# Attention without row maxima: a runtime bound on the scores, a factor table in place of bias matmuls, and a branch to the general program

## The chip, the cores and the metric

The kernel runs on one core of a Trainium2 chip. A core has TensorE (PE, matmuls; PEld is its weight loads), VectorE (DVE), ScalarE (ACT), GpSimd (POOL) and SyncE (SP, which issues most DMAs). Matmuls read SBUF and write PSUM, which has eight banks of 512 float32 columns here. The metric is device microseconds of one launch; lower is better.

## The reference

One encoder layer on x of 1024 tokens by 1024, float32. One projection gives q, k, v of two head groups, which run side by side; then an output projection, and a gated MLP with a depthwise convolution over positions.

```python
def rms_norm(x, g): return x * rsqrt(mean(x * x) + 1e-6) * g

# mixer A: 8 query heads, 2 key heads of 64, all 1024 keys
qa, ka = rope(rms_norm(qa, qa_norm_g)), rope(rms_norm(ka, ka_norm_g))
p = softmax(qa @ ka.T / 8);  out_a = p @ va
# mixer B: 8 heads; patterns (window, dilation) (128,1), (512,4), (2048,16), merged by their denominators
sc = rms_norm(qb, qb_norm_g) @ rms_norm(kb, kb_norm_g).T / 8 - slope[h] * distance      # -1e30 outside
w = softmax(logsumexp of each pattern);  out_b = sum of w * softmax(sc) @ vb
x = x + concat(rms_norm(out_a), rms_norm(out_b)) @ w_out
x = x + conv_ffn(rms_norm(x))
# qa_norm_g, ka_norm_g, qb_norm_g, kb_norm_g: 64 values each, 1 + 0.05 * normal
```

After the norms a q or k vector of 64 is no longer than 8 times its largest gain, so a score is at most 8 times the product of the two largest gains.

## The kernel before

The kernel is written with the Tile framework: Python emits the operations in an order written out by hand, and the framework's planner then sets each engine's queue, and may move an operation ahead of others. SBUF is two arenas, `bigf` (float32) and `bigr` (fp32r, the format of the fast matmuls), addressed by fixed offsets; PSUM is `ps`. For precision an operand is split into a high and a low fp32r part, and a product is the sum of high x high, high x low and low x high.

The stages follow one another in time: the input projection (to about 208 us), mixer A (208 to 426), mixer B (426 to about 578, its end mixed with the output projection), the output projection to about 665, the up-projection with convolution and gate, and the down-projection.

**Mixer A** takes 16 groups `g`, each one block of 128 positions and one key head, whose four query heads make 512 columns. `a_main` walks eight key tiles `kt`: two score matmuls of 512 columns (lines 664 and 665) into bank 2 or 3, an exp on ACT from PSUM to SBUF (667), and two tiles later the product with V (line 659, plain float32, four pieces, each two passes in the trace). Between them it takes the next group's preparation from a list: `nat` (split of q, 616 and 617), `first` (four transposes and a copy), `mx(i)` four times, and `last`, which turns the maxima into columns. The weights of line 664 stack K's high and low part in 128 partitions against q's high part twice; those of line 665 stack K's high part with rows of -1 against q's low part and the row maximum, so the score arrives with its maximum subtracted. Transposes all show at line 177 or 180.

```python
635  for hf in range(2):
637      mm(bank(hf), r(q2 + 128 * i, 128), r(R_K2A + 1024 * kv + 512 * hf, 512), start=True, stop=True)
638      vec.tensor_reduce(f(SM_MC + 8 * hf + i, 1), bank(hf), axis=AX.X, op=OP.max)
```

**Mixer B** takes 8 heads of 8 steps `s` in one loop: `b_s(h, s)` makes scores, `b_pv` two steps later the product with V. Steps 0 to 3 are banded (near keys that are not a multiple of 4 away), steps 4 to 7 strided (keys 4 apart, all three patterns together, each key counted as often as it occurs). A bias matmul with the identity (line 793) first writes the table of distance penalties, `tbc`, into the bank; then two pairs of 256-column score matmuls (805 and 807, or 815 and 816), again with the maximum in the second; an exp in PSUM (819); for banded steps a high part (ACT, 821) and a low part (DVE, 822), for strided steps a product with the count table `cnt` (824). Sums of V products are gathered at 844 and 848 and normalised at 684 and 685. In the same steps run the next head's preparation: `b_split` (split of k and q, 720, 721, 616, 617), `trq` and `trk` (transposes and copies), `mx(tt)` eight times (a 432-column and a 256-column product, lines 753 to 758, each with a masked maximum on DVE against the table `tmx`, line 764), and `trl` (772 to 777). Head 0's preparation runs in A's last two groups.

```python
793  bias = lambda o, rhs, first: mm(o, r(R_IDR, 128), rhs, start=first, stop=False, skip_group_check=True)
819  act(bank(st), bank(st), AF.Exp)
821      act(r(ph, 512), bank(st), AF.Copy)
822      vec.tensor_tensor(r(pl, 512), bank(st), rf(ph, 512), op=OP.subtract)
824      vec.tensor_tensor(heads(f(p, 512), 2), heads(bank(st), 2), fp(F_CNT, [128, 2], [1, 256]), op=OP.mult)
```

`load_tmx` (SP queue, 672 KB) and `load_tabs` (POOL queue, 384 KB) fetch the two tables once a head. POOL also copies K's high part to other partitions by a DMA (740).

Of the kernel before, what the change touches and what calls it, by code (L numbers as in the profile page):

```python
# [20 lines left out]
HD = 64  # L21
# [19 lines left out]
NF = O_F + 9232  # L41
# [49 lines left out]
F_CNT = O_F + 8720  # L91

# [31 lines left out]
def tile_encoder_layer(ctx, tc, x, w_in, gains, outg, norm1_g, norm2_g, w_out, w_up, conv_w, conv_b,  # L124
                       w_down, ident, rope, tmx, tbc, cnt, out):
# [13 lines left out]
    act = nc.scalar.activation  # L139
    vec = nc.vector  # L140
    gp = nc.gpsimd
    mm = nc.tensor.matmul
    dma = nc.sync.dma_start

    def f(off, n):
        return bigf[:, off:off + n]

    def r(off, n):
        return bigr[:, off:off + n]

    def rf(off, n):
        return bigr[:, off:off + n].bitcast(F32)

    def raw_ap(base, dims):
        return bass.AP(tensor=base.tensor, offset=base.offset,
                       ap=[list(base.ap[0])] + [list(d) for d in dims])

    def fp(off, *dims):
        return raw_ap(bigf[:, off:off + 1], dims)

    def rp(off, *dims):
        return raw_ap(bigr[:, off:off + 1], dims)

    def rfp(off, *dims):
        return raw_ap(bigr[:, off:off + 1].bitcast(F32), dims)

    def pp(off, *dims):
        return raw_ap(PS[:, off:off + 1], dims)

    def bank(i, n=512, o=0):  # L170
        return PS[:, 512 * i + o:512 * i + o + n]

    def heads(ap, n):
        return ap.rearrange("p (h d) -> p h d", h=n)

    def tr_r(b, slot, src):
        nc.tensor.transpose(bank(b, 128, 128 * slot).bitcast(F32R), src, r(R_IDR, 128))

    def tr_f(b, slot, src):
        nc.tensor.transpose(bank(b, 128, 128 * slot), src, f(O_IDF, 128))  # L180

    def perm_rows(t, b, width):
        rr, c = divmod(b, 2)
        return bass.AP(tensor=t.tensor, offset=t.offset + (512 * c + rr) * width, ap=[[4 * width, 128], [1, width]])

    def bcast(t, n, off=0):
        return bass.AP(tensor=t.tensor, offset=t.offset + off, ap=[[0, 128], [1, n]])

    def newton(dst, v, root, t):

        vec.reciprocal(root, root)
        vec.tensor_tensor(t, root, root, op=OP.mult)
        vec.scalar_tensor_tensor(t, t, -0.5, v, op0=OP.mult, op1=OP.mult)
        vec.scalar_tensor_tensor(dst, t, 1.5, root, op0=OP.add, op1=OP.mult)

    trb = [0]

    def next_tr():
        trb[0] ^= 1
        return 4 + trb[0]  # L200

    def evac_split(o, b, n=512):
        act(r(o, n), bank(b, n), AF.Copy)
        vec.tensor_tensor(r(o + 1024, n), bank(b, n), rf(o, n), op=OP.subtract)

    def xt(tt):
        return R_XT + 2048 * tt

    def qab(tt):
        return O_QAB + 1024 * tt  # L210

    def fill(dst, n, m, c, src=O_IDF, eng=None):

        src = f(src, m)[:, None, :].to_broadcast([128, n, m])
        if eng is None:
            vec.tensor_scalar(dst, src, 0.0, c, op0=OP.mult, op1=OP.add)
        else:
            act(dst, src, AF.Copy, scale=0.0, bias=c)
# [5 lines left out]
    INW = 2304  # L224
    chunks = [(1280, "kb"), (1792, "vb"), (0, "qa"), (768, "qb")]
    prods = [(c, n) for c in range(4) for n in ((1, 5, 2, 7, 6, 3, 4) if c else (1, 2, 5, 7, 6, 3, 4))]

    def a_op(n, t):
        return R_A[n] + 1024 * t

    def split(o, src):
        act(r(o, 512), src, AF.Copy)
        vec.tensor_tensor(r(o + 512, 512), src, rf(o, 512), op=OP.subtract)

    def x_bank(tt):
        return 4 + 2 * (tt % 2)

    def x_prep(tt):
        for half in range(2):
            b = x_bank(tt) + half  # L240
            for k in range(4):
                tr_f(b, k, f(qab(tt) + 512 * half + 128 * k, 128))
            split(a_op(((1, 2), (3, 4))[tt // 4][half], tt % 4), bank(b))

    def x_rest(tt):
        q0, q1 = qab(tt % 4), qab(tt % 4 + 4)
        b = x_bank(tt), x_bank(tt) + 1
        act(f(F_JNK, 512).bitcast(BF), f(qab(tt), 1024), AF.Square, accum_out=f(SM_SS1 + tt, 1))
        vec.tensor_scalar(f(SM_E1 + tt, 1), f(SM_SS1 + tt, 1), EPS / D, EPS * EPS, op0=OP.mult, op1=OP.add)
        if tt < 4:  # L250
            for half in range(2):
                act(f(q0 + 512 * half, 512), bank(b[half]), AF.Copy)
        else:
            act(f(q1, 512), bank(b[0]), AF.Copy)
            vec.tensor_tensor(f(q1 + 512, 512), f(q0, 512), bank(b[0]), op=OP.subtract)
            vec.tensor_tensor(f(q1, 512), bank(b[1]), f(q1, 512), op=OP.add)
            gp.tensor_tensor(f(q0, 512), f(q1, 512), f(q0, 512), op=OP.subtract)
            gp.tensor_tensor(f(q0 + 512, 512), f(q0 + 512, 512), f(q0, 512), op=OP.subtract)

    def s_split(n, t):  # L260
        raw = {5: qab(t + 4), 7: qab(t + 4) + 512, 6: qab(t), 3: qab(t) + 512}[n]
        split(a_op(n, t), f(raw, 512))


    def kv_load(half):
        src = bass.AP(tensor=w_in.tensor, offset=w_in.offset + 512 + 512 * half * INW,
                      ap=[[INW, 128], [128 * INW, 4], [1, 256]])
        dma(heads(f(F_WC + 1024 * half, 1024), 4), src)

    def kv_split(k):  # L270
        o, raw, g = R_A[7] + 2048 * (k // 4) + 256 * (k % 4), f(F_WC + 256 * k, 256), f(SM_G1 + k, 1)
        act(r(o, 256), raw, AF.Copy, scale=g)
        vec.scalar_tensor_tensor(r(o + 1024, 256), raw, g, rf(o, 256), op0=OP.mult, op1=OP.subtract)

    def kv_bank(tt):
        return tt if tt < 4 else 2 + tt % 2

    def kv_proj(tt):
        for k in range(8):
            a = a_op(((1, 2), (3, 4))[tt // 4][k // 4], tt % 4) + 128 * (k % 4)  # L280
            w = R_A[7] + 2048 * (k // 4) + 256 * (k % 4)
            o = bank(kv_bank(tt), 256)
            mm(o, r(a, 128), r(w, 256), start=(k == 0), stop=False)
            mm(o, r(a, 128), r(w + 1024, 256), start=False, stop=False)
            mm(o, r(a + 512, 128), r(w, 256), start=False, stop=(k == 7))

    def rot(dst, qn, nh, tab):
        for half in range(2):
            gp.tensor_tensor(fp(dst + 16 * half, [64, nh], [32, 2], [1, 16]),
                             fp(qn + 16 * (1 - half), [64, nh], [32, 2], [1, 16]),  # L290
                             fp(tab + 64 + 16 * half, [0, nh], [32, 2], [1, 16]), op=OP.mult)

    def kv_out(i):
        stg = F_KVT + 256 * (i % 3)
        act(f(stg, 256), bank(kv_bank(i), 256), AF.Copy)  # L295
        dma(kvscr[i], f(stg, 256))


    def k_fetch():
        dma(heads(f(F_TMP, 1024), 8), kvscr[:, :, 0:128].rearrange("t p c -> p t c"))  # L300

    def k_norm():
        k3, t = heads(f(F_TMP, 1024), 16), F_KSQ + 1024
        act(f(F_KSQ, 1024), f(F_TMP, 1024), AF.Square)
        vec.tensor_reduce(f(t, 16), heads(f(F_KSQ, 1024), 16), axis=AX.X, op=OP.add)
        vec.scalar_tensor_tensor(fp(t + 16, [2, 8], [1, 2]), fp(t, [2, 8], [1, 2]), 1.0 / HD,
                                 fp(SM_E1, [1, 8], [0, 2]), op0=OP.mult, op1=OP.add)
        act(f(t + 32, 16), f(t + 16, 16), AF.Sqrt)
        newton(f(t, 16), f(t + 16, 16), f(t + 32, 16), f(t, 16))
        vec.tensor_tensor(k3, k3, f(t, 16)[:, :, None].to_broadcast([128, 16, 64]), op=OP.mult)  # L310
        vec.tensor_tensor(k3, k3, fp(O_GA + 128, [0, 16], [1, 64]), op=OP.mult)

    def k_turn():
        for ax in range(2):
            for half in range(2):
                gp.tensor_tensor(fp(F_KSQ + 32 * ax + 16 * half, [128, 8], [64, 2], [1, 16]),
                                 fp(F_TMP + 32 * ax + 16 * (1 - half), [128, 8], [64, 2], [1, 16]),
                                 fp(F_ROPE + 64 + 32 * ax + 16 * half, [128, 8], [0, 2], [1, 16]), op=OP.mult)

    def k_add():  # L320
        k4 = fp(F_TMP, [128, 8], [64, 2], [1, 64])
        vec.tensor_tensor(k4, k4, fp(F_ROPE, [128, 8], [0, 2], [1, 64]), op=OP.mult)
        vec.tensor_tensor(f(F_TMP, 1024), f(F_TMP, 1024), f(F_KSQ, 1024), op=OP.add)
# [815 lines left out]
    for t in tail:  # L1139
        t()  # L1140
# [433 lines left out]
```

## Time and profile before

| | |
|---|---|
| median of 3 runs | 1325.74 us (1324.68 to 1325.79) |
| span of the profiled execution | 1324.9 us (its own time beyond the span is not given) |
| granted TensorE clock, mean | 0.998 |
| PE / DVE / ACT / POOL busy | 1298.4 / 1013.5 / 682.2 / 387.2 us |
| mixer A, window 208 to 426 | PE busy 218.0, DVE 131.0, ACT 112.9 us |
| mixer B, window 426 to 578 | PE busy 145.4, DVE 117.5, ACT 112.5 us |

A row of a group of instructions reads: line, engine, operation, output<-input by the program's names, shape of output<-input, xcount | busy us, mean ns of one | idle time of the engine just before them and what ended it. A matmul's duration overlaps the next one's, so its cost on the queue is the distance to the next start. A row of the timeline starts with the start in us and the length in us. A row of a window lists busy time and count of each engine, then the granted clock, the DMA share and GB/s.

### The profile page before, as it was taken

How to read it: one execution, taken by the hardware profiler on the slowest of the kernel's cores; microseconds unless marked ns; L12 is line 12 of the kernel's file. 1: busy time of each engine (PE TensorE's matmuls, PEld its weight loads, DVE VectorE, ACT ScalarE, POOL GpSimd, SP SyncE). 2: the span in 40 equal slices, each digit the busy share in tenths (PEclk: the TensorE clock that was granted, in tenths of full speed). 3: DMA queues.
4: the chain of work that ended last, by engine and by line, in shares of the span. 5: the costliest groups of instructions: out<-in, count | busy, mean ns of one | idle time of the engine just before them, and what ended most of it. 6: DMA issues, size and time to landing. Idle time of an engine off the chain costs nothing.

```text
span 1324.9 us, 20107 instructions
## 1 busy us (share of the span) xinstructions
PE 1298.4 (98%) x7559; PEld 1127.1 (85%) x7559; DVE 1013.5 (76%) x1599; ACT 682.2 (51%) x1070; POOL 387.2 (29%) x304
## 2 busy tenths in 40 slices
PE   8999999999999999999999999999999999999998
PEld 7999999999999888878877888888888888888887
DVE  4987687556655777866588999999999999586674
ACT  8855564555545777773465444444544445244331
POOL 1611122000111222100115667656766653100000
PEclk9999999999999999999999999999999999999999
DMA  7145211001002455333222222322232225897873
GB/s 259 53 113 127 81 44 48 17 1 35 4 9 66 98 141 143 97 118 111 82 70 88 103 104 103 111 96 97 88 119 104 104 95 191 307 309 232 293 232 104
DMA packets 120500, 152.28 MB, mean 115 GB/s; under 512 B 50962, under 2 KB 77010, under 8 KB 119890
## 3 DMA queue, kind: packets, MB, share of 16 engines
q1 hardware_dynamic: 118609, 143.65, 33.3%
q0 software_dynamic: 1792, 7.34, 2.5%
q8 instruction: 59, 0.97, 0.3%
q14 instruction: 40, 0.32, 0.1%
HBM read 112.95 MB, written 33.82 MB: 111 GB/s over the span
## 4 chain that ended last, share of the span: by engine, by line
PE 77%; DVE 14%; issue 4%; ACT 4%; DMA 1%; SPq 0%; DVEq 0%; ACTq 0%
PE ps L659 8%; DVE bigf L1288 6%; PE ps L1255 6%; PE ps L1257 6%; PE ps L1256 6%; PE ps L1387 5%; PE ps L1386 5%; PE ps L1388 5%; PE ps L411 3%; PE ps L412 3%; PE ps L413 3%; PE ps L664 3%; PE ps L637 2%; PE ps L665 2%; DVE bigf L1259 2%
## 5 line engine op out<-in xcount | busy, mean ns | idle before, releaser
L1255 PE MATMUL ps<-bigr 128*128 128x512 f32 x616 | 241.6, 392 | 6.3 <-DVE bigf L1259 5.7
L1256 PE MATMUL ps<-bigr 128*128 128x512 f32 x616 | 240.4, 390 | 0.0
L1257 PE MATMUL ps<-bigr 128*128 128x512 f32 x616 | 240.3, 390 | 0.0
L1288 DVE SCALAR_TENSOR_TENSOR bigf<-bigf 128x768 f32<-128x768 f32 (+1 forms) x176 | 178.7, 1073 | 26.5 <-ACT bigf L1286 26.3
L1238 ACT ACTIVATE bigr<-bigf 128x512 fp32r<-128x512 f32 x154 | 93.2, 625 | 139.2 <-POOL bigf L1230 70.3
L659 PEld LDWEIGHTS ps<-bigf 128*128 128x128 f32 x1024 | 139.9, 191 | 10.3
L1255 PEld LDWEIGHTS ps<-bigr 128*128 128x128 f32 x616 | 116.0, 188 | 35.0 <-DVE bigf L1259 9.1
L1366 ACT ACTIVATE bigr<-bigf 128x1024 fp32r<-128x1024 f32 x77 | 80.7, 1060 | 119.1 <-PE ps L1388 65.7
L1257 PEld LDWEIGHTS ps<-bigr 128*128 128x128 f32 x616 | 116.0, 188 | 24.4
L1256 PEld LDWEIGHTS ps<-bigr 128*128 128x128 f32 x616 | 116.0, 188 | 23.6
L659 PE MATMUL ps<-bigf 128*128 128x65 f32 x1024 | 135.2, 267 | 0.0
L411 PE MATMUL ps<-bigr 128*128 128x256 f32 x448 | 127.2, 284 | 1.2 <-ACT bigf L295 1.2
L1239 DVE TENSOR_TENSOR bigr<-bigf,bigr 128x512 fp32r<-128x512 f32 x112 | 125.2, 1135 | 3.2 <-ACT bigr L1238 2.7
L412 PE MATMUL ps<-bigr 128*128 128x256 f32 x448 | 126.8, 283 | 0.0
L413 PE MATMUL ps<-bigr 128*128 128x256 f32 x448 | 126.7, 283 | 0.0
L667 ACT ACTIVATE bigf<-ps 128x512 f32<-128x512 f32 x128 | 76.0, 597 | 94.5 <-PE ps L665 93.4
L1387 PE MATMUL ps<-bigr 128*128 128x512 f32 x308 | 119.9, 389 | 0.0
L1388 PE MATMUL ps<-bigr 128*128 128x512 f32 x308 | 119.8, 389 | 0.0
L1386 PE MATMUL ps<-bigr 128*128 128x512 f32 x308 | 119.8, 389 | 0.0
L1367 DVE TENSOR_TENSOR bigr<-bigf,bigr 128x1024 fp32r<-128x1024 f32 x77 | 93.0, 1222 | 27.1 <-ACT bigr L1366 23.2
L638 DVE TENSOR_REDUCE bigf<-ps 128x1 f32<-128x512 f32 x128 | 86.3, 690 | 23.5 <-PE ps L637 21.6
L411 PEld LDWEIGHTS ps<-bigr 128*128 128x128 f32 x448 | 85.8, 192 | 1.9 <-ACT bigf L295 1.6
(233 smaller groups left out, 2860.2 us busy)
## 6 DMA issues: line engine op xcount, KB each, us to landing
bigf<-w_down SPq DMA_DIRECT2D x99, 256.0 KB, 4.5
bigf<-w_up SPq DMA_DIRECT2D x44, 512.0 KB, 3.6
bigf<-gscr SPq DMA_DIRECT2D x77, 256.0 KB, 4.2
gscr<-bigf SPq DMA_DIRECT2D x33, 512.0 KB, 2.6
bigf<-w_in SPq DMA_DIRECT2D x8, 1024.0 KB, 5.2
bigf<-x SPq DMA_DIRECT2D x15, 512.0 KB, 6.5
bigf<-tmx SPq DMA_DIRECT2D x8, 672.0 KB, 5.2
bigf<-w_out SPq DMA_DIRECT2D x8, 512.0 KB, 5.9
```

Of the source, the lines that this page charges most:

```text
L411: mm(o, ah, wh, start=(k == 0 and t % 2 == 0 and n != 2), stop=False, skip_group_check=True)
L412: mm(o, ah, wl, start=False, stop=False, skip_group_check=True)
L413: mm(o, al, wh, start=False, stop=(k == 3), skip_group_check=True)
L659: mm(bank(ob, 65, 66 * i), f(slots[kt] + 128 * i, 128), f(F_VA + 132 * kt + 66 * kv, 65), start=(kt == 0 and i == 0), stop=(kt == 7), skip ...
L1239: (gp if n in (2, 4) and m > 3 else vec).tensor_tensor(rp(o + 512, [128, 4], [1, 128]), src, rfp(o, [128, 4], [1, 128]), op=OP.subtract)
L1255: mm(bank(b), wh, th, start=(k == 0 and n in (1, 5, 6, 7)), stop=False, skip_group_check=True)
L1256: mm(bank(b), wh, tl, start=False, stop=False, skip_group_check=True)
L1257: mm(bank(b), wl, th, start=False, stop=(k == 3), skip_group_check=True)
L1288: vec.scalar_tensor_tensor(f(a + o, n), f(i + d, n), w_, f(a + o, n), op0=OP.mult, op1=OP.add)
L1386: mm(o, ah, r(d, 512), start=(q == 0 and n in (1, 5, 2)), stop=False, skip_group_check=True)
L1387: mm(o, ah, r(d + 1024, 512), start=False, stop=False, skip_group_check=True)
L1388: mm(o, al, r(d, 512), start=False, stop=(q == NQ - 1), skip_group_check=True)
```

## The change

The body of the program becomes a function, emitted twice: `emit(True)`, and, behind a branch at run time, `emit(False)`, which is the program of before. `emit(True)` works out from the gains the square of a bound on any score, 64 times the larger of max(qa gain squared) x max(ka gain squared) and max((qb gain x kb gain) squared), and leaves maxima out: exp of the bare scores. If the bound exceeds 256 (scores over 16), it multiplies the q gains by 0, so that nothing overflows, and the branch at its end runs the general program over it.

- **Scores.** K is stacked as low and high part, q as high and low part, so the first score matmul gives low x high and high x low; the second is high x high, its other 64 weight rows zero. The counts of matmuls stay, `mx`, `last`, `trl`, the bias matmuls and the transposes of the maxima go. `k_ready` moves K's high part down by a POOL DMA instead of an ACT copy.
- **Tables.** `tee` = exp(`tbc`) times the counts, 768 columns a head, loaded in two halves of 192 KB on SP's queue. One DVE product after exp replaces the bias matmul and, in strided steps, the count product. In banded steps it writes float32 to SBUF; high part (`tensor_copy`) and low part both follow on DVE.
- **Banks.** Score banks rotate over 2, 3, 0, 1 instead of 2, 3.
- Three output weights load to another place, since `tee` lies where they lay.

The diff, without its whitespace and cut:

```diff
+    def emit(bounded):
 def k_split():
-    act(rp(R_KNA, [128, 16], [1, 64]), src, AF.Copy)
-    vec.tensor_tensor(rp(R_KNA + 64, ...), src, rfp(R_KNA, ...), op=OP.subtract)
+    h, l = (64, 0) if bounded else (0, 64)
+    act(rp(R_KNA + h, [128, 16], [1, 64]), src, AF.Copy)
+    vec.tensor_tensor(rp(R_KNA + l, ...), src, rfp(R_KNA + h, ...), op=OP.subtract)
 def k_ready(u):
     act(rp(R_K2A + 256 * u, [128, 2], [1024, 2], [1, 128]), pb, AF.Copy)
+    if bounded:
+        gp.dma_start(rp(R_KHA + 256 * u, [1024, 2], [1, 256])[0:64], rp(R_K2A + 256 * u, [1024, 2], [1, 256])[64:128])
+        return
     act(rp(R_KHA + 256 * u, [128, 2], [1024, 2], [1, 128])[0:64], pb[0:64], AF.Copy)
+def bound():
+    t = F_UA
+    vec.tensor_tensor(fp(t, [64, 2], [1, 64]), fp(O_GA, [128, 2], [1, 64]), fp(O_GA, [128, 2], [1, 64]), op=OP.mult)
+    vec.tensor_tensor(f(t + 128, 64), f(O_GB, 64), f(O_GB + 64, 64), op=OP.mult)
+    vec.tensor_tensor(f(t + 128, 64), f(t + 128, 64), f(t + 128, 64), op=OP.mult)
+    vec.tensor_reduce(f(t + 192, 3), heads(f(t, 192), 3), axis=AX.X, op=OP.max)
+    vec.tensor_tensor(f(t + 192, 1), f(t + 192, 1), f(t + 193, 1), op=OP.mult)
+    vec.tensor_tensor(f(t + 192, 1), f(t + 192, 1), f(t + 194, 1), op=OP.max)
+    vec.tensor_scalar(f(O_LIM, 1), f(t + 192, 1), float(HD), None, op0=OP.mult)
+    vec.tensor_scalar(f(O_LIM + 1, 1), f(O_LIM, 1), LIMIT, None, op0=OP.is_le)
 def late_consts():
+    if bounded:
+        bound()
...
+            vec.tensor_scalar(f(g, 64), f(g, 64), HD ** -0.5, f(O_LIM + 1, 1), op0=OP.mult, op1=OP.mult)
+def q_pair(src, stride, eng, n, o):
+    q = fp(src, [stride, n], [1, 64])
+    act(rp(R_QD + o, [128, n], [1, 64]), q, AF.Copy)
+    eng.tensor_tensor(rp(R_QD + 64 + o, [128, n], [1, 64]), q, rfp(R_QD + o, [128, n], [1, 64]), op=OP.subtract)
 def a_prep(g):
+    if bounded:
+        return [nat, first]
     return [nat, first] + [lambda i=i: mx(i) for i in range(4)] + [last]
 def a_main(g, prep, tail, late, plan, late_plan):
-        st = 2 + kt % 2
+        st = (2, 3, 0, 1)[kt % 4] if bounded else 2 + kt % 2
-        mm(bank(st), r(R_KHA + 1024 * kv + 128 * kt, 128), r(ql, 512), start=False, stop=True)
+        mm(bank(st), r(R_KHA + 1024 * kv + 128 * kt, 128), r(q2 if bounded else ql, 512), start=False, stop=True)
+def load_tee(h, part):
+    if bounded and h < 8:
+        dma(f(F_TEE[part], 384), tee[h][:, 384 * part:384 * part + 384])
 def b_prep(h):
+    if bounded:
+        return [[L(trq, 0)], [L(trk, 0), L(trk, 1)]], \
+            [[L(trq, 1)], [], [], [], [L(b_split, h + 1) if h < 7 else None], [], [], []]
+def b_s_bounded(h, s):
+    st = (2, 3, 0, 1)[s % 4]
...
+        for i, k in enumerate(ks):
+            mm(o, r(k, 128), q, start=(u == 0 and i == 0), stop=(i == 1), skip_group_check=True)
+    p, ph, pl = b_slots[h, s] = p_slots()
+    act(bank(st), bank(st), AF.Exp)
+    if s >= 4:
+        vec.tensor_tensor(heads(f(p, 512), 2), heads(bank(st), 2), fp(tb, [128, 2], [1, 256]), op=OP.mult)
+        return
+    at = [ta + win(2 * s + u) - 32 * (2 * s + u) + 32 for u in range(2)]
+    if at[0] == at[1]:                                   # s = 1, 2
+        vec.tensor_tensor(fp(p, [256, 2], [64, 4], [1, 64]), pp(512 * st, [256, 2], [64, 4], [1, 64]),
+                          fp(at[0], [0, 2], [96, 4], [1, 64]), op=OP.mult)
+    else:                                                # s = 0, 3
+        for u in range(2):
+            vec.tensor_tensor(fp(p + 256 * u, [64, 4], [1, 64]), pp(512 * st + 256 * u, [64, 4], [1, 64]),
+                              fp(at[u], [96, 4], [1, 64]), op=OP.mult)
+    vec.tensor_copy(r(ph, 512), f(p, 512))
+    vec.tensor_tensor(r(pl, 512), f(p, 512), rf(ph, 512), op=OP.subtract)
 # the loop of mixer B
         b_s(h, s)
+        if s == 4:
+            load_tee(h + 1, 0)
+        if s == 0 and h:
+            load_tee(h, 1)
...
+emit(True)
+limit = nc.values_load(bigf[0:1, O_LIM:O_LIM + 1].bitcast(mybir.dt.int32), ...)
+with tc.If(limit > int(np.float32(LIMIT).view(np.int32)), preferred_fallthrough_block=False):
+    emit(False)
```

More of the change, by code (lines that the diff above doesn't have):

```diff
@@ L158, in fp @@
[L158 to L177, printed above, removed]
@@ L245, in x_rest @@
[L245 to L258, printed above, removed]
@@ L287, in rot @@
[L287 to L300, printed above, removed]
@@ L313, in k_turn @@
[L313 to L323, printed above, removed]
@@ new lines, in emit @@
+        last = NPAIR - 1
+        for m in range(len(steps)):
+            n, q = steps[m]
+            down(m)
+            d_prep(m + 3)
+            if m < 2:
+                conv(last, m)
+            if m == 2:
+                gate(last, 0)
+                gate(last, 1)
+            if m == 3:
+                take(gate_sums(last), 4)
+            d_load2(m + 6)
+            d_load(m + 7)
+            behind(n, q)
+    emit(True)
+    limit = nc.values_load(bigf[0:1, O_LIM:O_LIM + 1].bitcast(mybir.dt.int32), min_val=0, max_val=2 ** 31 - 1,
+                           skip_runtime_bounds_check_because="any float32 that is not negative is right")
```

2257 lines of the change are left out of this document (1163 added, 1094 removed).

## The prediction

> **What bounds the kernel now.** I read the page first: the busy line and the chain of waits.
>
> ```profile
> PE 1298.4 (98%) x7559; PEld 1127.1 (85%) x7559; DVE 1013.5 (76%) x1599; ACT 682.2 (51%) x1070; POOL 387.2 (29%) x304
> ...
> PE 77%; DVE 14%; issue 4%; ACT 4%; DMA 1%; SPq 0%; DVEq 0%; ACTq 0%
> ```
>
> TensorE holds 98% of the span and 77% of the chain. The change cuts TensorE work out of two stages, so I next asked for busy time by window: mixer A (208 to 426), one head of mixer B (464 to 483), the last head, and everything from the up-projection on, which the change leaves alone.
>
> ```profile
> 208.00:426.00 218.00, 218.00 (x1574) 200.32 (x1573) 130.96 (x268) 112.91 (x192) 23.62 (x27) 1.00 0.08 22
> 464.00:483.00 19.00, 18.33 (x141) 16.13 (x140) 14.86 (x49) 13.67 (x26) 4.96 (x5) 1.00 0.50 128
> 559.00:578.00 19.00, 17.51 (x119) 14.61 (x118) 14.25 (x22) 15.17 (x26) 0.00 (x0) 1.00 0.40 125
> 665.00:1325.00 660.00, 647.70 (x2845) 531.42 (x2842) 549.44 (x617) 282.70 (x368) 275.86 (x194) 1.00 0.44 147
> ```
>
> The columns are PE, PEld, DVE, ACT and POOL busy. In A, TensorE never rests and the others are at 60% or less: a matmul removed is time removed. In a B head TensorE has 18.33 of 19.00 us, but DVE has 14.86 and ACT 13.67, so what is saved there ends where one of these takes over. The granted clock is 1.00 in all four.
>
> The profiled execution spans 1324.9 us; its own time beyond the span is not given, but the runs' median is 1325.74, so some 0.8 us lies around a span. I subtract from the median. About 0.2% (2.6 us) is what a measurement can tell from no change.
>
> **Mixer A.** Removed per group: eight max matmuls (line 637) with their DVE reductions (638), and four of eight transposes (643) with one ACT copy. The scores stay at two matmuls per key tile. The timeline of TensorE shows what a key tile costs:
>
> ```profile
> 303.64 0.48 PE L664 MATMUL ps<-bigr 128*128 128x512 f32 x1
> 303.96 0.40 PE L665 MATMUL ps<-bigr 128*128 128x512 f32 x1
> 304.19 0.63 PE L637 MATMUL ps<-bigr 128*128 128x512 f32 x2
> 304.65 1.00 PE L659 MATMUL ps<-bigf 128*128 128x65 f32 x8
> 305.46 0.47 PE L664 MATMUL ps<-bigr 128*128 128x512 f32 x1
> ```
>
> Durations overlap, so I count from start to start. From 303.64 to 305.46 is 1.82 us; the two max matmuls hold 304.19 to 304.65, 0.46; without them a tile is 1.36 us. Four transposes I read from
>
> ```profile
> 493.55 0.54 PE L177 MATMUL ps<-bigr 128*128 128x128 f32 x4 [0.67 <-DVE bigr L772]
> 493.92 0.35 PE L758 MATMUL ps<-bigr 128*128 128x256 f32 x1
> ```
>
> as 0.37 us. After the change A has 128 tiles (174.1), 15 sets of q transposes (5.6) and 16 transposes for B's first head (1.4): 181.1 us against 218.0, which is 36.9 less. The first group's max matmuls lie ahead of the window: 8 x 0.23 + 0.37 = 2.2 more. Together **39.1**. No other engine becomes late: per tile of 1.36 us ACT has one exp of 0.6. Four score banks instead of two, and two tiles between an exp and its use (2.7 us), cover the exp. The copy of K's high part to the lower partitions becomes four POOL transfers (`k_ready`); on POOL's queue they stand behind the rotary products, three of them also behind one table product, and ahead of the rest of the late norm work. The last two products of the last chunk (48 matmuls of 0.12 us each, as below) lie between them and the first score, so I cost them at nothing; without that cover it is one small transfer's landing, 2 us.
>
> **Mixer B, heads 0 to 6.** Off TensorE go, per head, the max matmuls (8 x (432 + 256) = 5,504 columns, lines 753 to 758), the bias matmuls (line 793, 8 x 512 = 4,096 columns) and eight transposes. The pace:
>
> ```profile
> 476.32 0.28 PE L815 MATMUL ps<-bigr 128*128 128x256 f32 x1
> 476.44 0.28 PE L816 MATMUL ps<-bigr 128*128 128x256 f32 x1
> ```
>
> 0.12 us for 256 columns: 2.6 + 1.9 us, and 0.74 for the transposes, so 5.2; and the 0.67 us wait for the last maximum (L772, the row above) goes too. TensorE's path becomes 19.0 - 5.9 = 13.1 us, if its other small waits stay.
>
> DVE loses the masked maxima and gains the factor products. One head before:
>
> ```profile
> L764 DVE CUSTOM_DVE_ANT_1 bigf<-ps,bigf 128x432 bf16<-128x432 f32 x8 | 4.8, 599 | 2.8 <-PE ps L757 1.7 <-PE ps L754 1.1
> L764 DVE CUSTOM_DVE_ANT_0 bigf<-ps,bigf 128x256 bf16<-128x256 f32 x8 | 3.3, 417 | 0.1
> L824 DVE TENSOR_TENSOR bigf<-ps,bigf 128x512 f32<-128x512 f32 x4 | 2.7, 687 | 0.6 <-ACT ps L819 0.6
> L822 DVE TENSOR_TENSOR bigr<-ps,bigr 128x512 fp32r<-128x512 f32 x4 | 2.7, 687 | 0.3 <-ACT bigr L821 0.2
> L848 DVE TENSOR_TENSOR bigf<-ps,bigf 65x512 f32<-65x512 f32 x3 | 2.1, 685 | 0.4 <-PE ps L841 0.4
> L764 DVE DVE_READ_ACCUMULATOR2_ANT bigf<- 128x1 f32 x16 | 1.3, 82 | 0.0
> ```
>
> The three L764 groups are 9.4 us. Added for the four banded steps: two products of 512 columns at 0.687 (as L824), four of 256 at 0.417 (as the 256-wide L764), four copies to fp32r, and the subtraction, which now reads two SBUF operands instead of one. These copies and subtractions have their prices here:
>
> ```profile
> L1239 DVE TENSOR_TENSOR bigr<-bigf,bigr 128x512 fp32r<-128x512 f32 x112 | 125.2, 1135 | 3.2 <-ACT bigr L1238 2.7
> ...
> L973 DVE TENSOR_TENSOR bigr<-bigf,bigr 128x512 fp32r<-128x512 f32 x12 | 7.9, 685 | 1.3 <-ACT bigr L972 1.3
> ...
> L216 DVE TENSOR_SCALAR bigr<-bigf 128x512 fp32r<-128x512 f32 x1 | 0.4, 418 | 0.0
> ```
>
> A copy is between 0.42 (L216, one SBUF operand) and 0.69 (L973); I take 0.42, the nearer form. The subtraction of two SBUF operands costs 0.685 in L973 and 1.135 in L1239, the stage where POOL works the most; I take 0.685. Added: 1.4 + 1.7 + 1.7 = 4.8. DVE: 14.86 - 9.4 + 4.8 = 10.3 us, and 13 if the copies and subtractions all cost their upper price. The four banded and four strided steps share that unevenly: 1.9 us each for the former (product, copy, subtraction), 0.69 for the latter.
>
> The Trainium skill, "SBUF — State Buffer", section "SBUF: two separate sides", says that VectorE with two SBUF inputs, or in a two-port mode, takes a port pair that GpSimd also uses, held for a whole instruction while the other blocks. L1239 against L973 agrees; by that rule POOL's three products a head would each hold up one of these new operations, for which the sum would be some 3 us more a head, as in the first rival.
>
> ACT drops the copies of the high part (it moves to DVE), the copies of the transposed maxima, and half of a 1024-column copy:
>
> ```profile
> L819 ACT ACTIVATE ps<-ps 128x512 f32<-128x512 f32 x8 | 4.8, 595 | 3.3 <-PE ps L816 2.4 <-PE ps L807 1.0
> L821 ACT ACTIVATE bigr<-ps 128x512 fp32r<-128x512 f32 x4 | 2.4, 602 | 0.1
> ```
>
> 13.67 - 2.4 - 1.2 (two more at 0.6) - 0.5 = 9.6 us. So TensorE remains the longest path at 13.1, with DVE at 10.3 to 13. What a banded step needs in series is 0.28 (last score) + 0.6 (exp) + 0.83 (two half products) + 0.42 + 0.69 = 2.8 us, against two steps of TensorE, 3.3 us: just covered. I add 0.4 for DVE's uneven load and take **13.5 us** a head: 7 x (19.0 - 13.5) = **38.5**. The factor table brings 2 x 192 KB a head where two tables brought 1,056 KB; its loads wait for the last product that reads the old half, four steps ahead of need. Behind them on SP's queue stand the loads of v and k for later heads, which have as much time.
>
> **Head 7** has no next head's maxima to lose. TensorE loses 1.9 us of bias; DVE gains 4.8 on 14.25 of 19. I take 0, between -1.9 and +3.
>
> **The ends.** `bound` adds eight small DVE operations, each like L591, where DVE idles:
>
> ```profile
> 24.80 0.15 DVE L249 TENSOR_SCALAR bigf<-bigf 128x1 f32<-128x1 f32 x1 [1.90 <-ACT bigf L248]
> ...
> L591 DVE TENSOR_SCALAR bigf<-bigf 128x64 f32<-128x64 f32 x2 | 0.4, 191 | 0.0
> ```
>
> 8 x 0.19 = 1.5 us into a hole of 1.9: 0.3, at most 1.5. At the end each engine loads the bound into a register and jumps over the general program's code. No row shows a jump that far. The nearest are
>
> ```profile
> q8 instruction: 59, 0.97, 0.3%
> ...
> bigf<-ident SPq DMA_DIRECT2D x1, 64.0 KB, 2.0
> ```
>
> code arrives by DMA in 16 KB packets, and a small transfer from memory lands after 2.0 us. Between 0 (hidden behind the output's landing) and 4.0 (two of them in series) I take 2.0. The Trainium skill, "Runtime: NRT & Kernel Launch", section "Instruction fetch mechanics", speaks against this part: prefetch is sequential, and a taken branch out of the current window stalls for a DMA fetch. By that rule the sum keeps its 2.0, and without it loses them.
>
> **Sum:** 1325.7 - 39.1 - 38.5 - 0 + 0.3 + 2.0 = 1250.4. I predict **1250 us**.
>
> **Rivals.** *DVE takes B over.* Eight new SBUF-only operations a head meet POOL's products. If each of the eight is lengthened by the 0.45 us between L973 and L1239, DVE reaches 10.3 + 3.6 = 13.9 us, and the banded steps, 2.4 us each instead of 1.9, outlast TensorE's 1.6; with TensorE in order behind them, the head is some 16 us (four steps at 2.4 and four at TensorE's 1.6). It decides where DVE's banded step exceeds 1.7 us. For it: L1239's mean. Against: POOL works 5 of 19 us here. Time: 7 x 3.0 = 21.0, so 1325.7 - 39.1 - 21.0 + 2.3 = 1268.
>
> *TensorE runs dense in B.* With two more score banks its remaining waits go. The floor is the series above shared over two steps, 2.8 / 2 x 8 = 11.2 us a head: 7 x 7.8 = 54.6, so 1325.7 - 39.1 - 54.6 + 2.3 = 1234. For it: A, where nothing waits. Against: three engines then stand within 2 us of each other.
>
> *The general program runs too (slower).* The branch compares the bits of one float in SBUF with those of 256. If the bound comes out above it, the whole old program follows: 1250 + 1325 = 2575. It decides at a product of squared gains of 256 / 64 = 4, gains of 1.41 in both vectors. The reference draws them as 1 + 0.05 times a normal, so 1.41 is eight deviations off; only a clobbered cell would do it.
>
> **How the numbers follow.** Forecast 0.64, DVE-bound 0.20, dense 0.13, both programs 0.02, anything else no faster 0.01. The range 1233 to 1274 goes from the dense case (with 1.5 us off for a head 7 that gains) to the DVE case with head 7's 3 us and both ends at their upper price (3.2 more). Faster by over 0.2%: 0.64 + 0.20 + 0.13 = 0.97, of which I keep 0.96 for errors in A; same 0.01; slower 0.03.
>
> **What would show it.** A: 181 us, a tile at 1.36, TensorE without idle. B: L764 and L793 gone, heads at 13.5 us, DVE about 10.3 of it, the SBUF subtraction at 0.69; at 1.1 the first rival holds. The stage from the up-projection on: 660 us as before. The last product to the end: about 2 us longer. Wrong would be: A above 190 (a wait I missed), heads at 16 or more, or over 5,000 more matmuls at the end.

## The result, and the profile after

The changed kernel takes 1300.74 us (four runs, 1300.09 to 1301.01) against 1325.76 us: 0.9814 of the time, with an interval of 0.98 to 0.9828. It is faster by 25 us where 75.7 were forecast, and 27 us above the top of the range. In the profiled execution after (span 1298.7 us) the busy line and the shares of the chain of waits read

```profile
PE 1236.4 (95%) x7063; PEld 1061.5 (82%) x7063; DVE 908.5 (70%) x1270; ACT 637.4 (49%) x1001; POOL 391.8 (30%) x300
...
PE 55%; DVE 18%; issue 4%; DMA 4%; ACT 3%; POOL 1%; SPq 0%; ACTq 0%; DVEq 0%; POOLq 0%
```

The second program did not run: 496 matmuls fewer, not 5,000 more. But TensorE holds 55% of the chain instead of 77%. Busy time by window shows where, with the columns PE, PEld, DVE, ACT, POOL, clock, DMA share, GB/s. The rows are mixer A, one head of mixer B, all from the first score of B to the end of the output projection, the up-projection and the down-projection:

```profile
210.40:391.60 181.20, 181.20 (x1366) 169.01 (x1364) 41.56 (x98) 101.92 (x180) 23.22 (x27) 1.00 0.07 18
411.60:426.50 14.90, 13.53 (x107) 11.47 (x107) 11.91 (x25) 10.31 (x20) 4.44 (x5) 1.00 0.53 121
391.60:616.00 224.40, 210.76 (x1300) 174.06 (x1298) 166.31 (x357) 129.99 (x260) 40.69 (x33) 0.98 0.40 109
616.00:1047.70 431.70, 423.57 (x1859) 346.70 (x1857) 399.91 (x441) 198.50 (x279) 262.75 (x186) 1.00 0.29 102
1047.70:1286.90 239.20, 221.19 (x925) 174.41 (x924) 139.44 (x154) 76.65 (x73) 10.77 (x6) 0.97 0.63 213
```

Against the same two last windows before:

```profile
677.60:1111.00 433.40, 425.22 (x1860) 347.91 (x1859) 399.95 (x442) 198.51 (x279) 262.50 (x186) 1.00 0.30 103
1111.00:1320.90 209.90, 209.88 (x925) 173.13 (x923) 138.98 (x154) 76.85 (x73) 10.76 (x6) 1.00 0.72 241
```

The down-projection, whose source lines are untouched, does the same work (925 matmul records in either window) in 239.2 us instead of 209.9; TensorE rested for none of it before and rests for 18 us now. When it began, the change was 63.3 us ahead; 29 of them are lost there. By stage, in us, from first matmul to first matmul of the profiled executions (the third measured column is a variant explained below):

| stage | before | forecast | after | row length kept |
|---|---|---|---|---|
| to A's first score product | 208.3 | 206.4 | 210.4 | 205.7 |
| mixer A | 217.9 | 181.1 | 181.2 | 181.0 |
| mixer B and output projection | 251.4 | 212.9 | 224.4 | 221.5 |
| up-projection | 433.4 | 433.4 | 431.7 | 431.8 |
| down-projection | 209.9 | 209.9 | 239.2 | 210.0 |
| from there to the end | 4.0 | 6.0 | 11.8 | 10.0 |
| span | 1324.9 | 1249.7 | 1298.7 | 1260.0 |

What TensorE waits for in the down-projection is said by the waits of that window. After the change (columns: total us, times, longest):

```profile
ACT bigr L1460 <- DMA bigf<-gscr: 57.1, 17, 12.2
...
PE ps L1480 <- ACT bigr L1460: 16.4, 8, 4.9
```

Before, TensorE has no wait in that window, and the waits of ScalarE are

```profile
ACT bigr L1366 <- PE ps L1388: 65.7, 40, 1.7
ACT bigr L1366 <- DVE bigf L1356: 28.0, 13, 3.6
ACT bigr L1366 <- DMA bigf<-gscr: 19.8, 7, 12.0
```

L1460 (L1366 before) is the copy of a step's operands to their high parts. Before, it waited mostly for TensorE, for a buffer to come free, which means that it ran ahead of need; now it waits most for loads, and TensorE for it. A long pause also costs more than itself:

```profile
1080.15 0.39 PE L1482 MATMUL ps<-bigr 128*128 128x512 f32 x1
1085.47 0.80 PE L1480 MATMUL ps<-bigr 128*128 128x512 f32 x1 [4.93 <-ACT bigr L1460]
```

After 4.93 us of waiting a matmul of the same shape takes 0.80 instead of 0.39. The granted clock is 0.50 for 6.8 us from 1084.0 on, when TensorE still waits, and for 3.4 us each from 1107.9 and 1138.6; in the 3.4 us ahead of these three stretches TensorE was busy 0.00, 1.79 and 1.39 us. Over the stage the clock is 0.97, and TensorE's busy time for the same matmuls is 11.3 us more than before.

### The profile page after: what moved, and what is told of

It reads as the page before. It is cut to its first block, busy times and chain, and to the rows that moved or that the text cites. A ratio compares the mean times of both kernels' runs of the same rounds, so it can differ in the third digit from the quotient of the medians.

```text
span 1298.7 us, 18774 instructions
## 1 busy us (share of the span) xinstructions
PE 1236.4 (95%) x7063; PEld 1061.5 (82%) x7063; DVE 908.5 (70%) x1270; ACT 637.4 (49%) x1001; POOL 391.8 (30%) x300
## 4 chain that ended last, share of the span: by engine, by line
PE 55%; DVE 18%; issue 4%; DMA 4%; ACT 3%; POOL 1%; SPq 0%; ACTq 0%; DVEq 0%; POOLq 0%
PE ps L696 8%; PE ps L1349 6%; PE ps L1351 6%; PE ps L1350 6%; DVE bigf L1382 6%; PE ps L1481 4%; PE ps L1482 4%; PE ps L1480 4%; PE ps L701 3%; PE ps L702 2%; DVE bigf L1353 2%; PE ps L1004 2%; PE ps L1006 2%; PE ps L1005 2%; DVE bigr L1333 2%
## 5 line engine op out<-in xcount | busy, mean ns | idle before, releaser
L1460 ACT ACTIVATE bigr<-bigf 128x1024 fp32r<-128x1024 f32 x77 | 80.5, 1058 | 148.9 <-DMA bigf<-gscr 57.1
L1349 PEld LDWEIGHTS ps<-bigr 128*128 128x128 f32 x616 | 115.6, 188 | 35.1 <-DVE bigf L1353 9.3
L696 PEld LDWEIGHTS ps<-bigf 128*128 128x128 f32 x1024 | 131.9, 191 | 9.3 <-issue 0.3
L1351 PEld LDWEIGHTS ps<-bigr 128*128 128x128 f32 x616 | 115.6, 188 | 24.2
L1350 PEld LDWEIGHTS ps<-bigr 128*128 128x128 f32 x616 | 115.7, 188 | 23.5
L696 PE MATMUL ps<-bigf 128*128 128x65 f32 x1024 | 129.1, 269 | 0.0
L421 PEld LDWEIGHTS ps<-bigr 128*128 128x128 f32 x448 | 85.8, 192 | 1.8 <-ACT bigf L300 1.6
L422 PEld LDWEIGHTS ps<-bigr 128*128 128x128 f32 x448 | 85.9, 192 | 0.3 <-DVE bigr L405 0.3
```

What stands on the lines that cost most here:

```text
L421: mm(o, ah, wh, start=(k == 0 and t % 2 == 0 and n != 2), stop=False, skip_group_check=True)
L422: mm(o, ah, wl, start=False, stop=False, skip_group_check=True)
L696: mm(bank(ob, 65, 66 * i), f(slots[kt] + 128 * i, 128), f(F_VA + 132 * kt + 66 * kv, 65), start=(kt == 0 and i == 0), stop=(kt == 7), skip ...
L1349: mm(bank(b), wh, th, start=(k == 0 and n in (1, 5, 6, 7)), stop=False, skip_group_check=True)
L1350: mm(bank(b), wh, tl, start=False, stop=False, skip_group_check=True)
L1351: mm(bank(b), wl, th, start=False, stop=(k == 3), skip_group_check=True)
```

## The experiments

What could make an untouched stage slower? One line of the change that the diff above does not show is

```diff
-NF = O_F + 9232
+NF = O_F + 9240
+O_LIM = O_F + 9232
```

`NF` is the row length of the arena `bigf`, 18,256 columns before and 18,264 after; the 8 new ones hold the bound. In the program, 148 of the 296 transfers that SP issues from the up-projection on stand at another place of its queue than before. A load of half a row of the residual (L1467, before L1373) that stood 89th stands 193rd, for instance. Two theories: the longer row does it (the planner takes accesses to conflict that don't), or it is a consequence of the faster mixers and the second program.

**The row length alone.** The kernel before, `NF` as after:

```diff
-NF = O_F + 9232
+NF = O_F + 9240
```

> The kernel before with one edit: its f32 arena has 8 more columns (as the change gives it), which nothing uses; everything is computed as before. Theory 'row length': with the longer row the planner takes the early load of one half row of the residual (L1373, into C_12) to conflict with reads of other columns and puts another order on SP's queue for the whole down-projection, the same order as in the changed kernel; so the down-projection goes from 209.4 to about 239 us and the time from 1325.8 to about 1355 us (1348 to 1360). Rival 'consequence of the mixer': the 29 us come from what the change does earlier (transfers that start at another time, the clock, the second program's code); then 8 unused columns cost nothing, 1325.7 (within 1.5).

Measured: 1363.35 us, 1.028 of before (1.0263 to 1.0297; the kernel before took 1325.95 beside it). Eight columns that nothing uses cost 37.4 us. The down-projection is nearly as in the changed kernel:

```profile
1116.60:1359.00 242.40, 224.48 (x925) 178.95 (x923) 139.61 (x154) 76.66 (x73) 10.77 (x6) 0.95 0.64 210
```

and A starts at 215.5 instead of 208.3, which the expectation had not foreseen: the input projection suffers too. There TensorE's transposes wait for ScalarE's copies of the transposed keys, as they do after the change; before, this wait is not among TensorE's. The waits of TensorE from 190 us on, up to A's start, in this kernel, then in the changed one:

```profile
PE ps L177 <- ACT bigr L337: 3.4, 2, 3.0
```

```profile
PE ps L182 <- ACT bigr L342: 2.6, 1, 2.6
```

In this kernel the granted clock is 0.50 for 6.8 us behind that wait (from 198.0 on), which adds to the delay.

**The change without the longer row.** The last 16 columns of the old row are used by nothing, so the bound fits there:

```diff
-NF = O_F + 9240
-O_LIM = O_F + 9232
+NF = O_F + 9232
+O_LIM = O_F + 9224
```

> The changed kernel with the bound's two cells in columns that were already free, so that the arena keeps the row length it had; everything else as changed. 'Row length': the order of the down-projection on every engine is that of the kernel before, its 238.8 us fall to about 209.5 and the time from 1300.7 to about 1271 us (1268 to 1275). 'Consequence of the mixer': the down-projection stays at about 239 and the time at 1300.

Measured: 1264.24 us (1261.92 to 1266.12), 0.9541 of before (0.9525 to 0.9557). 36.5 us come back, more than expected: in the profiled executions the input projection gains 4.7 as well, mixer B 2.9 (its granted clock is 1.00 here and 0.98 after the change) and the tail 1.8. The row of the down-projection is that of before again:

```profile
1040.00:1250.00 210.00, 209.93 (x925) 173.09 (x923) 138.38 (x154) 76.87 (x73) 10.77 (x6) 1.00 0.73 241
```

**Sixteen columns fewer.**

```diff
-NF = O_F + 9232
+NF = O_F + 9216
```

> The kernel before with a row of 18,240 columns, 16 fewer than it had (its last 16 were unused). Theory 'the row length has to be a multiple of 16 columns': the planned order is that of the kernel before and the time too, 1325.7 (within 1.5). Rival 'any other length than the tuned one costs': 1350 or more.

Measured: 1325.74 us, 1.0002 of before (0.9993 to 1.0012). So it is not any change of the length. In the planned program, lengths of 18,240 and 18,256 columns give one order of SP's queue from the up-projection on, and 18,248, 18,252, 18,257, 18,258, 18,260, 18,262 and 18,264 give others. The two are multiples of 16 columns, the others not. Of these, three lengths were timed.

**The order alone.** The kernel before with its own row, SP's queue put into the other order by links that set order and wait for nothing (`rec` holds the 296 transfers as the program emits them, `SP_ORDER` their places in the other order, in runs of neighbours):

```diff
+    line = [rec[s + i] for s, n in SP_ORDER for i in range(n)]
+    for u, v in zip(line, line[1:]):
+        tc.add_manual_dep(v, u.name, mybir.DependencyInfo(mybir.DependencyClass.NoSync, ...), ...)
```

> The kernel before with its own row length; only the order in which SP issues the 296 transfers from the up-projection on is set, by order-only links, to the order that the longer row gave (148 of 296 places differ). Theory 'order': the queue order alone makes the down-projection slow, 209.4 to about 240 us and 1325.8 to about 1357 us (1350 to 1363); the input projection, which is left alone, stays at 208.3. Rival 'waits': the longer row also adds real waits of instructions on other engines for transfers, and the order by itself costs a third or less: 1326 to 1336.

Measured: 1333.56 us, 1.0064 (1.0047 to 1.008). The down-projection takes 217.5 us, with 4.5 us of idle TensorE:

```profile
1109.70:1327.20 217.50, 213.02 (x925) 173.93 (x923) 138.24 (x155) 76.17 (x73) 10.76 (x6) 0.99 0.71 234
```

The order explains 7.6 of the 29 to 33 us, less than a third, as the rival had it. That the rest is real waits follows only by exclusion here; the next run tests it.

**The reads of two pieces.** In 22 steps the operand copies read two distant pieces of the arena by one access of two dimensions. The long row stays, and these steps (`n` 5 and 6) get one-piece reads:

```diff
+if bounded and n in (5, 6):
+    for i, s in enumerate((t, o + 512)):
+        act(r(d + 512 * i, 512), f(s, 512), AF.Copy)
+        ...
+    return
 src = fp(t, [o + 512 - t, 2], [1, 512]) if n in (5, 6) else fp(o, [512, 2], [1, 512])
 act(rp(d, [512, 2], [1, 512]), src, AF.Copy)
```

> The changed kernel with its long row; only the two instructions of a down-projection step that read two distant pieces at once (L1460 and L1461 for products 5 and 6, 22 of 77 steps) are made as two instructions of one piece each. Theory 'false conflicts of the two-piece reads': with the longer row the planner holds such a read to conflict with loads into other columns, so ScalarE waits for transfers issued much later than its own; one-piece reads are free of that, the down-projection goes from 238.8 to about 211 us (44 more short instructions a few of which may show) and the time from 1300.7 to about 1273 us (1269 to 1278); the input projection stays late (A starts at 210 to 211). Rival 'the long row does it through all accesses': the down-projection stays above 230, 1295 or more.

Measured: 1270.04 us (1267.71 to 1272.57), 0.9582 (0.9565 to 0.9599). The down-projection is at full pace with the long row:

```profile
1048.10:1257.70 209.60, 209.60 (x925) 173.30 (x924) 140.06 (x176) 79.74 (x95) 10.76 (x6) 1.00 0.72 241
```

A still starts late, at 210.5. So the 29 us of the down-projection are shown to come from those 22 reads under the longer row. The run also rules out that the longer row costs them on the chip itself, by where it puts the data: the row here is as long. In the program they are tied to loads into columns that they don't read: the load of line 1467 named above goes to columns 1,536 to 2,047 of the work area and stands behind such reads of other columns, 193rd; in the program of this run it stands 89th again. How the planner compares two accesses, and which accesses of the input projection it ties, stays open.

**The branch.** The changed kernel without the last lines:

```diff
-limit = nc.values_load(bigf[0:1, O_LIM:O_LIM + 1]...)
-with tc.If(limit > ...):
-    emit(False)
```

> The changed kernel without the load of the bound into registers, the branch and the general program behind it (bound and all the rest are kept). Theory 'the branch costs all of the tail': from the last product to the end 12.2 us become the 4.5 of the kernel before, 1300.7 - 7.7 = 1293 us. Rival 'the branch costs what was forecast': about 2 us go, 1298.7, the rest of the tail is the last output rows landing late. Rival 'row length in another guise': the down-projection also changes when the second program is gone; by the planned order it should not, 239 us in either case.

Measured: 1294.3 us (1293.34 to 1296.22); from the last product to the end 4.1 us instead of 11.8, the down-projection still 239.2. The branch costs 6 to 8 us, three to four times the forecast. What is in it can be read from the instructions of its lines on SP's queue, in the version with the row length kept, where SP issues its last output transfer until 1251.1:

```profile
L1610 SPq TENSOR_LOAD <-bigf x1: 523/523/523, 1251.2 to 1251.2; - x1
...
L1612 SPq EVENT_SEMAPHORE  x8: 17/17/17, 1254.7 to 1255.7; - x8
L1612 SPq COMPARE_BRANCH  x2: 43/46/49, 1251.8 to 1255.8; - x2
...
L1672 SPq EVENT_SEMAPHORE  x14: 17/28/28, 1258.4 to 1260.0; - x14
```

The columns are durations in ns, then the first and last start in us. The load takes 0.5 us. The first branch stands at 1251.8 and the next instruction at 1254.7: 2.9 us. The second branch stands at 1255.8 and the next instruction at 1258.4: 2.6 us. There are two far jumps in series, to a short block of eight semaphore updates and from there to the end. The price is not the same on every queue: in the same trace the first jump took 0.1 us on VectorE's (1251.0 to 1251.1) and 0.6 on ScalarE's, the second 3.3 and 2.6. What sets it is not shown. To save one jump the general program was placed directly behind the branch:

```diff
-with tc.If(limit > ..., preferred_fallthrough_block=False):
+with tc.If(limit > ..., preferred_fallthrough_block=True):
```

> The narrow version (1264.2 us) with the general program placed directly behind the branch, so that the way past it is one far jump, where the trace shows two on SP's queue (2.9 us to the short block, 2.6 us from it to the end). Theory 'each far jump is a fetch': one of them goes, 1264.2 - 2.6 = 1261.6 us. Rival 'the load and the semaphore updates make the tail': no change, 1264.

Measured: 1260.21 us (1259.29 to 1261.86) against 1264.24, with one branch on SP's queue and 6.8 us from the last product to the end instead of 10.0. On SP's queue a far jump is worth some 3 us here.

**Mixer B: GpSimd's share.** A head takes 15.3 us on average after the change (18.9 before), not 13.5. The timelines of GpSimd and of VectorE at the turn of a head, after (start, length, instruction):

```profile
426.30 1.30 POOL L766 TENSOR_TENSOR bigr<-bigf,bigr 128x512 fp32r<-128x512 f32 x1 [1.32 <-ACT bigr L765]
427.57 1.72 POOL L651 TENSOR_TENSOR bigr<-bigf,bigr 128x512 fp32r<-128x512 f32 x1
```

```profile
425.86 0.42 DVE L906 CAST bigr<-bigf 128x512 fp32r<-128x512 f32 x1
426.19 0.68 DVE L900 TENSOR_TENSOR bigf<-ps,bigf 128x512 f32<-128x512 f32 x1
426.79 1.35 DVE L907 TENSOR_TENSOR bigr<-bigf,bigr 128x512 fp32r<-128x512 f32 x1
428.07 1.50 DVE L906 CAST bigr<-bigf 128x512 fp32r<-128x512 f32 x1
429.49 0.68 DVE L931 TENSOR_TENSOR bigf<-ps,bigf 65x512 f32<-65x512 f32 x1
430.09 0.68 DVE L907 TENSOR_TENSOR bigr<-bigf,bigr 128x512 fp32r<-128x512 f32 x1
```

The copy takes 0.42 and the subtraction 0.68 when GpSimd rests, 1.50 and 1.35 when it works; the product L900, which reads PSUM, takes 0.68 in any case. In the seven heads six of the 28 subtractions take 1.18 to 1.60 and four of the 28 copies 1.44 to 1.50; all ten overlap GpSimd's subtraction for k (L766) or for q (L651). The other 46 are at their price, but for one copy of 0.73. GpSimd's third, v's (L757), mostly falls on operations of VectorE that read PSUM, which are not lengthened. To see what that is worth, GpSimd's three subtractions were left out for heads 1 to 7:

```diff
-gp.tensor_tensor(rp(kl, ...), k3, rfp(kh, ...), op=OP.subtract)
+if h == 0 or not bounded:
+    gp.tensor_tensor(rp(kl, ...), k3, rfp(kh, ...), op=OP.subtract)
 ...
```

> The changed kernel, in which GpSimd's three subtractions per head (low parts of k, q and v, L757, L651, L766) are left out for heads 1 to 7, so that these low parts are stale; the work of TensorE, VectorE and ScalarE is unchanged. Theory 'GpSimd lengthens VectorE': the banded copies (L906) and subtractions (L907) that now take up to 1.5 us take 0.41 and 0.69, heads 0 to 6 of mixer B go from 15.6 us to about 13.9, and the time from 1300.7 to about 1289 us (1286 to 1292). Rival 'chain of the banded step': the heads are held by the series exp, product, copy, subtraction alone, whatever GpSimd does: heads at 15 or more, 1297 to 1301.

Measured: 1290.83 us (1289.75 to 1290.94), heads at 13.7 us, mixer B and output projection 212.8 where 212.9 was forecast. The groups of VectorE over mixer B, after the change and then in this kernel, where the copy and the subtraction stand at lines 909 and 910:

```profile
L907 DVE TENSOR_TENSOR bigr<-bigf,bigr 128x512 fp32r<-128x512 f32 x28 | 23.3, 831 | 0.0
L906 DVE CAST bigr<-bigf 128x512 fp32r<-128x512 f32 x28 | 16.3, 582 | 0.0
```

```profile
L910 DVE TENSOR_TENSOR bigr<-bigf,bigr 128x512 fp32r<-128x512 f32 x29 | 19.8, 684 | 0.0
L909 DVE CAST bigr<-bigf 128x512 fp32r<-128x512 f32 x28 | 11.8, 421 | 0.0
```

The theory of GpSimd holds: without its work the copy, the subtraction and the head come out close to the forecast (0.42, 0.685, 13.5).

Not all of the 1.6 us a head is GpSimd's. Over the seven heads the granted clock is 0.95 after the change and 1.00 in this run; the version with the row length kept has the same means of copy and subtraction (0.58 and 0.83), a clock of 1.00, and heads of 14.9 us. So GpSimd's work is worth some 1.2 us a head and the clock 0.4. Another way for GpSimd to cost time would be that TensorE waits for its results. After the change these waits are two of 0.9 us in the seven heads, of 11.4 us that separate the two kernels there.

**Keeping all of the work.** Two ways to take VectorE and GpSimd apart, both on the version with the row length kept (1264.24 us, heads 14.9). The first moves the copy:

```diff
-vec.tensor_copy(r(ph, 512), f(p, 512))
+act(r(ph, 512), f(p, 512), AF.Copy)
```

> The narrow version (1264.2 us), in which the copy of a banded step's factors to the high part (L906) is made by ScalarE instead of VectorE. Theory 'VectorE's banded step bounds mixer B': a banded step of VectorE loses 0.42 us and the copies that GpSimd lengthened to 1.4; heads from 15.3 to about 14, 1264.2 - 8 = 1256 us (1252 to 1260). Rival 'series': exp, product, a 0.6 us copy behind the next exp, and the subtraction make the step longer in series than two steps of TensorE cover: no gain, 1264 to 1270.

Measured: 1259.85 us (1259.0 to 1261.44), heads 14.2. The second moves two of GpSimd's subtractions to VectorE:

```diff
-gp.tensor_tensor(rp(dst + 66, ...), v3, rfp(dst, ...), op=OP.subtract)
+(vec if bounded else gp).tensor_tensor(rp(dst + 66, ...), v3, rfp(dst, ...), op=OP.subtract)
-q_pair(O_QAB + 512 + 64 * h, 1024, gp, 8, 0)
+q_pair(O_QAB + 512 + 64 * h, 1024, vec, 8, 0)
```

> The narrow version (1264.2 us), in which two of GpSimd's three subtractions per head (low parts of v, L766, and of q, L651) are made by VectorE at about 0.69 us each; GpSimd keeps k's. Theory 'GpSimd lengthens VectorE': VectorE gains 1.4 us of work a head and loses about 1.7 of lengthening, and TensorE no longer waits for the 1.3 to 1.7 us subtractions: heads at 14 to 14.8, 1264.2 - 6 = 1258 us (1254 to 1262). Rival 'VectorE is the bound by its sum': 1.4 us more on 12 of 15 us a head cost as much as they save, 1264 or above.

Measured: 1260.03 us (1259.76 to 1260.9), heads 14.4. The line of v's subtraction is L757, and L766 is k's; the expectation has them exchanged. In both the subtraction L907 still averages 0.79 to 0.83 us, since GpSimd keeps some work.

Then both together with the single far jump (the diffs of the three runs in one kernel):

> The three edits that each brought some 4 us to the narrow version (1264.2 us), together: the banded copies on ScalarE, the low parts of v and q on VectorE, one far jump at the end. If their gains add up: 1264.2 - 4.4 - 4.2 - 4.0 = 1251.6 us. If the first two are the same gain (both take VectorE and GpSimd apart): about 1256.

And k's subtraction on VectorE too:

```diff
-gp.tensor_tensor(rp(kl, ...), k3, rfp(kh, ...), op=OP.subtract)
+(vec if bounded else gp).tensor_tensor(rp(kl, ...), k3, rfp(kh, ...), op=OP.subtract)
```

> As the run before, and the low part of k on VectorE too, so that GpSimd has no product or subtraction in mixer B. Theory 'GpSimd lengthens VectorE': the subtraction (L907) is 0.69 us everywhere, heads at 13.7 as without GpSimd's work, 1249 to 1252 us. Rival 'VectorE full': 0.7 us more on VectorE costs what the last contention cost, 1252 to 1256.

Measured: 1256.17 us (1255.48 to 1256.88) and 1254.26 us (1251.5 to 1255.0). In the first, the gains of the two moves did not add up, heads are at 14.3. In the second, with nothing of GpSimd's beside it, VectorE's subtraction is back at its price, and heads are at 13.7:

```profile
L907 DVE TENSOR_TENSOR bigr<-bigf,bigr 128x512 fp32r<-128x512 f32 x31 | 21.0, 685 | 1.0 <-ACT bigr L906 0.8
```

By the heads, VectorE is not too full for 2.1 us more a head. By its time the run lies in the range of the rival (1252 to 1256) and not in that of the theory (1249 to 1252); 1.4 us of that is in the tail, 8.1 us against 6.7 in the run before. This last kernel, at 0.9454 of before (0.9438 to 0.947), beats both the kernel before and the changed one (1300.74).

## Why the prediction was wrong, step by step

**"The stage from the up-projection on: 660 us as before" failed**, and with it the range. It took an unchanged source for an unchanged program. The change alters the length of the arena's row, the planner reads that length, and the down-projection came out with other waits and another order of SP's queue: 29.3 us. The forecast did speak of SP's queue, but only at the loads of the table, not at what else the planner would make of the edit. With the row length kept the kernel takes 1264.2 us, inside 1233 to 1274.

**Input projection.** Forecast: 2.2 us off for the first group's maxima, 0.3 on for `bound`. Measured: 2.1 on. With the row length kept, A starts at 205.7 (206.3 to 207.0 in the five later versions that keep it), where 206.4 was forecast, so the step was right and some 4 us are the row's.

**Mixer A.** Right: 181.2 us against 181.1, and TensorE never rests in it. Start-to-start distances, a count of removed matmuls and a check of the other engines were enough, because no engine was near its limit.

**Mixer B.** The term was mis-sized: 38.5 us forecast, 27.0 measured, 29.9 with the row length kept, where the granted clock is 1.00. The removed and added operations were priced correctly one by one: 0.42 and 0.685 us are found where GpSimd rests. The failing step is "I take 0.685" for an operation whose upper price, 1.135 us, had been quoted with its reason, and "I take 0.42" beside it. The means were 0.83 and 0.58, together 1.2 us more a head.

The first rival had the mechanism and the wrong count. It lengthened all eight new operations by 0.45 us. In fact GpSimd's subtractions for k and q, at the turn of a head, lengthen one or two of the eight, by 0.5 to 1.1 us each, and leave the others alone. Its head of 16 us was nearer than 13.5 (15.3 measured, 14.9 at a clock of 1.00), but by a slip: eight times 0.45 us are 0.9 more for each banded step, so 2.8 us instead of 1.9, not 2.4, and a head of 17.6. Nor could its condition, a banded step of more than 1.7 us, tell the two cases apart, for the forecast's own banded step was 1.9. The measured one is 0.68 or 2 x 0.42 for the product, and 0.58 and 0.83 on average for the copy and the subtraction, 2.1 to 2.3 us.

The Trainium skill, "SBUF — State Buffer", section "SBUF: two separate sides", calls the port pair that the two engines share an exclusive lock held for the whole instruction. The trace agrees: VectorE's two long operations end at 428.14 and 429.57 us, 0.54 and 0.28 us behind the GpSimd operations that they met (427.60 and 429.29). The dense case did not come: heads are at 13.7 us even without GpSimd's work, not at 11.2.

**The tail.** 2.0 us forecast, at most 4.0; measured 7.8, or 6.0 with the row length kept. The bound of "two of them in series" was right in its count of two, and on SP's queue each costs 2.6 to 2.9 us, not 2.0; the register load and eight semaphore updates, 1.7 us more between them, were not in the sum. The Trainium skill, "Runtime: NRT & Kernel Launch", section "Instruction fetch mechanics", says that a taken branch out of the fetched window stalls for a fetch; the two gaps on SP's queue and the 3.2 us that one jump fewer saves agree with it.

**The second program** did not run, as forecast.

## What to carry to other kernels

An edit changes the program that the planner makes, not the lines that it touches: compare the queues of the stages that an edit "leaves alone" before calling them unchanged, and look first at what is shared by all of them, such as the row length of a buffer. Keep that length, or take another that leaves the queues as they were (a multiple of 16 float32 columns here), or read distant pieces by separate accesses. And price an operation on VectorE that reads SBUF only by what GpSimd does at that moment, not by an average of the stage.

## What was not expected of the hardware

- A far jump cost 2.6 and 2.9 us on SP's queue, though the general program behind the branch was not executed; on VectorE's queue one of the two cost 0.1.
- VectorE's copy of 128x512 with one SBUF operand, 0.42 us alone, took 1.50 beside a GpSimd subtraction; the product that reads PSUM was not lengthened.
- After 4.93 us without a matmul, TensorE ran the next one at half the pace (0.80 for 0.39 us). In the kernel after the change the granted clock was 0.50 in six stretches of 3.4 or 6.8 us ahead of its end, and in the 3.4 us before each of them TensorE had been busy 2.34 us or less. A stage with a few long waits thus lost more than the waits: in the kernel with only the longer row, the mean granted clock of the down-projection is 0.95. Whether so much rest always brings the lower clock is not shown.
